# First stage of a two-layer diffusion backbone: filter spectra in float32, squares summed on four strips, the norm of x applied apart from its modulation, loads in another order

## The chip, the cores and the metric

The kernel runs on one core of a Trainium2 chip. The metric is device time in microseconds of one execution, the median of several runs. A core has TensorE (PE in the views, with its weight loads as PEld), VectorE (DVE), ScalarE (ACT), GpSimd (POOL) and the DMA engines, which SyncE's queue (SP) and POOL's queue feed. PE writes to PSUM; DVE and ACT read PSUM and SBUF, POOL reads SBUF.

## The reference

Two layers over 512 latent tokens (`x`) and 256 context tokens (`ctx`), width 1024. Layer 0 is differential attention with an MLP, layer 1 a Hyena long convolution with an MLP. All is float32. Cut to what the first stage prepares:

```python
silu_c = jax.nn.silu(c)
mod_l = jnp.split((silu_c @ w_mod[i] + b_mod[i])[:, None, :], N_MOD, axis=-1)
u_l = modulate(rms_norm(h_lat, norm_mix_pre[i]), mod_l[0], mod_l[1])   # x*(1+scale)+shift
u_c = modulate(rms_norm(h_ctx, norm_mix_pre[i]), mod_c[0], mod_c[1])
y_l, y_c = differential_attention(u_l, u_c, ...)                       # layer 0
...
h = (hdn @ w_out).reshape(n, 2, D_MODEL)                               # filters of layer 1
h = h * jnp.exp(-t * deltas[None, :])[:, None, :]
kf = jnp.fft.rfft(kern, n=2 * n, axis=0)                               # their spectra
```

## The kernel before

Weights and activations that PE multiplies are split in a high and a low float32r half (`split`, L259 to L263: ACT writes the high half by a cast on L262, DVE or POOL the difference on L263), and `mm3` makes three products of them. The string `WLO` names for each kind of weight which engine takes the difference, "v" for DVE and "p" for POOL, in turn.

The first stage is the function `startup` (L436 to L650). Its steps are named by a letter: `F0` to `F2` the small filter network, `f` the filters of 512 channels by 128 positions (`filters`), `s` the four spectra (`spectra`, two halves each), `m` eight products of the modulation row (`mod0`), `n` squares and norms (`norms`), `x` and `c` the eight modulated and split rows of x and of ctx (`modsplit`). `SORDER` sets the order in which the steps are recorded, before and after the modulation vectors `mod` and `modc` are there; `DORDER` sets the order of the loads on SP. Of a tile with a tag there are as many buffers as `bufs` says (`mw0` has 8, so four steps of `mod0`; the PSUM tag `ps` has 5).

A scheduler then places every recorded instruction on its engine; the table `PRI` shifts the priority of each named part of the program, in all stages. Each engine works strictly in the order it was given.

Then come `proj_q` (its products are `ps_q`), `proj_k` (`ps_k`), `proj_kc` (`ps_kc`) and `values` (`ps_v`) of attention. `ps_q`, `ps_k`, `ps_kc` and `ps_v` take turns in two PSUM buffers (tag `pj`), so `ps_kc` needs the buffer of `ps_q` and `ps_v` that of `ps_k`. A buffer is free when `rotate` has read it, at last by `rr<-ps_q` on DVE (L677), which needs the table `rope`. `rope` and the loads `mw` of `mod_step` (256 KB each, two buffers, consumed by `macc` on DVE, L361 and L363) lie in memory that the first stage gives back with its last instruction on DVE, `nlam` (L650). Behind attention follow the MLP of layer 0, the Hyena layer and its MLP.

Of the kernel before, what the change touches and what calls it, by code (L numbers as in the profile page):

```python
# [32 lines left out]
for _name, _w in (  # L33
# [38 lines left out]
 'b.hid': -65,
 'b.mod': 207,
 'b.pre': -127,
 'b.res': -60,
 'b.wload': -203,
 'e.cbc': -258,
# [3 lines left out]
 'e.hid': 73,
 'e.mod': 178,
 'e.pre': 0,
 'e.res': 575,
 'e.wload': -370,
 'f.cbc': 20,
# [12 lines left out]
 'h.pre': 492,
 'h.res': 7,  # L100
 'h.tr': 238,
 'h.wload': 122,
 'hid': -139,
# [1 line left out]
 'm.hid': 0,
 'm.wload': 29,
 'res': -163,
 'rot': 0,
 's.chain': 60,
 's.wload': 40,  # L110
 'smx': 6,
 'val': -198,
 'wload': -209,
 'wpart': 74,
 'wt': 328}
WLO = dict(fil="vp", fdft="ppv", start="p", q="vpv", k="pv", v="p", wo0="vvp", wo7="v", wo1="vpp", w1f0="vpv", w1f1="vvvp", w1_0="vpv", w1_1="vvvp", w2_0="v", w2_1="vpp", w2l0="v", w2l1="vpp", hin0="pvv", hin="pvp", hout="pv")
# [116 lines left out]
class K:  # L233
# [202 lines left out]
    def startup(self, sp, pp, cp):  # L436
# [104 lines left out]
        hs, hdif = {}, {}  # L541

        def filters(g, tt):

            gs = slice(512 * g, 512 * g + 512)
            if tt == 0:
                if g:
                    room = [sp.tile([P, 2, 512], F32R, tag="mw0", name="hs", bufs=MW0) for _ in range(8)]
                    room = [[room[i // 2][:, i % 2] for i in range(j, j + 4)] for j in (0, 4, 8, 12)]
                else:  # L550
                    room = [sp.tile([P, 4, 512], F32R, tag="hs" + t, name="hs") for t in "hl"] + [
                        cp.tile([P, 4, 512], F32R, tag="c" + t, name="hd") for t in "hl"]
                    room = [[t[:, i] for i in range(4)] for t in room]
                hs[g], hdif[g] = room[0:2], room[2:4]
            dec = sp.tile([P, 512], F32, tag="dec", name="dec", bufs=2)
            nc.scalar.activation(dec, dlt[:, gs], AF.Exp, scale=tn[:, tt:tt + 1])
            for i, dst in ((0, hs[g]), (1, hdif[g])):
# [4 lines left out]
                self.split(ht, dst[0][tt], dst[1][tt], self.turn("fil"))

        def spectra(g, m):
            ms = slice(P * m, P * m + P)
            for cs, src in ((0, hs[g]), (1, hdif[g])):
                so = self.wp.tile([P, 2, 512], F32, tag=("whi", "wlo")[cs], name="so")
                pe = pp.tile([P, 512], F32, tag="ps", name="ps_e")
                po = pp.tile([P, 512], F32, tag="ps", name="ps_o")
                for par, ps in ((0, pe), (1, po)):  # L570
# [2 lines left out]
                ev = sp.tile([P, 512], F32, tag="ev", name="ev", bufs=4)
                nc.scalar.copy(ev, pe)
                eng = nc.vector
                if g:
                    ov = sp.tile([P, 512], F32, tag="ev", name="ov", bufs=4)
                    nc.scalar.copy(ov, po)
                    eng, po = nc.gpsimd, ov
                eng.tensor_add(so[:, 0], ev, po)  # L580
                if cs == 0:
                    eng.tensor_sub(so[:, 1], ev, po)
                else:
                    eng.tensor_sub(so[:, 1], po, ev)
                nc.gpsimd.dma_start(self.spec[m][g][:, 2 * cs:2 * cs + 2], so)
# [699 lines left out]
```

## Time and profile before

| | us |
|---|---|
| median of 3 runs (1501.72 to 1508.04) | 1502.05 |
| the profiled execution, its own time | 1503.08 |
| span of that execution, first to last instruction | 1501.3 |
| PE busy (94% of the span) | 1411.0 |
| DVE busy (64%) | 967.6 |
| ACT busy (44%) | 665.9 |
| POOL busy (21%) | 321.2 |

The time lies 1.8 us above the span and 1.0 above the median. A busy PE is not PE at its peak: the span of a matmul in the views covers its latency, so the price of one in a stream is read from the distance of two starts. Times within the span start at its first instruction.

### The profile page before, as it was taken

The page shows a single profiled execution, that of the slowest core. Times are in us where ns is not written, and L with a number is a line of the kernel's source. Part 1 is how long each engine was busy: PE and PEld are TensorE (multiplying, and loading weights), DVE is VectorE, ACT ScalarE, POOL GpSimd, SP SyncE. Part 2 cuts the span into 40 slices and gives each one's busy share as a digit, 9 for nine tenths or more (in the row PEclk, how much of TensorE's full clock was granted, in tenths as well). Part 3 has the DMA queues.
Part 4 walks back from the last instruction along what each step waited for, and adds up shares of the span by engine and source line. Part 5 has one row for each costly group of instructions (what it writes and reads, how often), then busy time and mean ns, then how long its engine had stood idle before and what let it go on. Part 6 is the DMA issues. An engine that isn't in the chain of part 4 may idle for free. (4 is left out here: it accounts for less than half of the span.)

```text
span 1501.3 us, 21240 instructions
## 1 busy us (share of the span) xinstructions
PE 1411.0 (94%) x8248; PEld 1218.3 (81%) x8248; DVE 967.6 (64%) x1658; ACT 665.9 (44%) x1175; POOL 321.2 (21%) x207
## 2 busy tenths in 40 slices
PE   6979999999997999999999999999999899999996
PEld 1559797878887988888888888888989788888896
DVE  5887887878577864656555686999787323233334
ACT  4555757567554543313222355443554423142332
POOL 2351201120213101010100224323422212131121
PEclk9989999999998999999999999999999999999998
DMA  9332232130142275655454022322321422222201
GB/s 332 154 126 99 85 113 85 65 104 29 55 170 99 86 239 195 211 196 181 151 179 149 29 85 91 134 71 99 113 75 53 141 98 98 84 99 99 98 29 57
DMA packets 58144, 174.76 MB, mean 116 GB/s; under 512 B 5787, under 2 KB 15387, under 8 KB 57788
## 3 DMA queue, kind: packets, MB, share of 16 engines
q1 hardware_dynamic: 56892, 169.22, 32.9%
q0 software_dynamic: 1152, 4.19, 0.7%
q8 instruction: 65, 1.06, 0.3%
q14 instruction: 35, 0.29, 0.1%
HBM read 167.10 MB, written 6.29 MB: 115 GB/s over the span
## 5 line engine op out<-in xcount | busy, mean ns | idle before, releaser
L263 POOL TENSOR_TENSOR wlo<-raw,whi 128x1024 fp32r<-128x1024 f32 x43 | 120.7, 2808 | 552.4 <-ACT whi L262 483.5
L262 ACT CAST whi<-raw 128x1024 fp32r<-128x1024 f32 x99 | 104.1, 1052 | 194.3 <-PE ps L285 98.6
L262 ACT CAST wxhi<-raw 128x1024 fp32r<-128x1024 f32 x92 | 96.8, 1052 | 204.4 <-PE ps L285 174.4
L263 POOL TENSOR_TENSOR wxlo<-raw,wxhi 128x1024 fp32r<-128x1024 f32 x33 | 80.4, 2438 | 299.6 <-ACT wxhi L262 299.6
L363 DVE SCALAR_TENSOR_TENSOR macc<-mw,silu,macc 128x1024 f32<-128x1024 f32 (+1 forms) x91 | 100.2, 1101 | 27.9 <-DMA mw<-in_wmod_dram 27.0
L263 DVE TENSOR_TENSOR wxlo<-raw,wxhi 128x1024 fp32r<-128x1024 f32 x59 | 73.3, 1243 | 63.2 <-ACT wxhi L262 63.1
L263 DVE TENSOR_TENSOR wlo<-raw,whi 128x1024 fp32r<-128x1024 f32 x56 | 69.6, 1243 | 66.6 <-ACT whi L262 66.5
L285 PE MATMUL ps<-hl,wxhi 128*128 128x512 f32 x240 | 95.7, 399 | 0.0
L286 PE MATMUL ps<-hh,wxlo 128*128 128x512 f32 x240 | 95.7, 399 | 0.0
L284 PE MATMUL ps<-hh,wxhi 128*128 128x512 f32 x240 | 95.4, 398 | 0.0
L284 PE MATMUL ps<-uh,wxhi 128*128 128x512 f32 x240 | 94.9, 396 | 0.0
L286 PE MATMUL ps<-uh,wxlo 128*128 128x512 f32 x240 | 94.7, 394 | 0.0
L285 PE MATMUL ps<-ul,wxhi 128*128 128x512 f32 x240 | 94.4, 393 | 0.0
L262 ACT CAST hh<-relu 128x512 fp32r<-128x512 f32 (+1 forms) x80 | 42.1, 536 | 78.5 <-DVE relu L947 78.2
L985 DVE TENSOR_TENSOR y<-y,ps 128x512 f32<-128x512 f32 x32 | 22.0, 686 | 82.1 <-PE ps L286 82.1
L263 DVE TENSOR_TENSOR hl<-relu,hh 128x512 fp32r<-128x512 f32 (+1 forms) x80 | 56.8, 718 | 27.4 <-ACT hh L262 27.0
L284 PE MATMUL ps_h<-uh,wxhi 128*128 128x256 f32 x240 | 68.5, 289 | 4.6 <-DVE relu L947 2.2
L947 DVE SCALAR_TENSOR_TENSOR relu<-ps,relu 128x512 f32<-128x512 f32 x48 | 33.0, 687 | 56.2 <-ACT relu L946 56.2
L815 ACT ACTIVATE p<-sc,mx 128x768 f32<-128x768 f32 x64 | 57.8, 905 | 24.6 <-DVE mx L813 22.1
L285 PE MATMUL ps_h<-ul,wxhi 128*128 128x256 f32 x240 | 68.4, 286 | 0.0
L286 PE MATMUL ps_h<-uh,wxlo 128*128 128x256 f32 x240 | 68.1, 285 | 0.0
L813 DVE TENSOR_REDUCE mx<-sc 128x1 f32<-128x768 f32 x64 | 60.8, 952 | 2.7 <-PE sc L810 1.8
(364 smaller groups left out, 4559.2 us busy)
## 6 DMA issues: line engine op xcount, KB each, us to landing
raw<-in_w_dram SPq DMA_DIRECT2D x128, 512.0 KB, 3.2
mw<-in_wmod_dram SPq DMA_DIRECT2D x72, 512.0 KB, 4.4
mw<-in_wmod_dram SPq DMA_DIRECT2D x48, 256.0 KB, 2.9
raw<-in_hin_dram SPq DMA_DIRECT2D x24, 512.0 KB, 3.2
raw<-in_wo_dram SPq DMA_DIRECT2D x11, 512.0 KB, 3.2
spec<-so POOLq DMA_DIRECT2D x8, 512.0 KB, 2.9
raw<-in_wq_dram SPq DMA_DIRECT2D x8, 512.0 KB, 3.2
raw<-in_wk_dram SPq DMA_DIRECT2D x8, 512.0 KB, 3.2
```

The source lines that it names most:

```text
L262: self.nc.scalar.copy(hi, src)
L263: (eng or self.nc.vector).tensor_sub(lo, src, hi.bitcast(F32))
L284: mm(ps, lhi, rhi, start=(start and i == 0), stop=False)
L285: mm(ps, lhi, rlo, start=False, stop=False)
L286: mm(ps, llo, rhi, start=False, stop=(stop and i == n - 1))
L363: nc.vector.scalar_tensor_tensor(acc, w, self.silu[:, kc:kc + 1], acc, op0=ALU.mult, op1=ALU.add)
L813: nc.vector.tensor_reduce(mx, sc[:, 0:768], axis=AX.X, op=ALU.min)
L815: nc.scalar.activation(p, sc[:, 0:768], AF.Exp, scale=-1.0, bias=mx, accum_out=s1 if mp else s0[:, qb:qb + 1])
L947: nc.vector.scalar_tensor_tensor(r[:, 0:n], ps, 0.0, r[:, 0:n], op0=ALU.max, op1=ALU.mult)
L985: nc.vector.tensor_add(y[:, mt], y[:, mt], ps)
```

## The change

Filters and spectra are kept in float32: `filters` writes `hs` straight from PSUM, `dft` is loaded without a split, and each spectrum takes 8 float32 products where it took 24 of float32r halves. The sums and differences `so` are all on DVE, from PSUM. The squares of x and ctx go to PE by 24 products with a matrix of ones on four strips of 32 columns (`bcs`), ACT copies the strips to `rows`, and the six products of `rstd` sum them; the tree of DVE additions goes. x and ctx are multiplied by the reciprocal norm as soon as it is there, before the modulation is; `modsplit` then has two ACT instructions and a subtraction on DVE. `mw0` has 6 buffers. The tables `PRI`, `WLO`, `DORDER` and `SORDER` change, those of `PRI` and `WLO` in all stages.

```diff
-WLO = dict(fil="vp", fdft="ppv", start="p", q="vpv", k="pv", v="p", wo0="vvp", wo7="v", ... w1f0="vpv", w1f1="vvvp", ... hin0="pvv", hin="pvp", hout="pv")
+WLO = dict(fil="pp", fdft="vvpp", start="p", q="v", k="v", v="v", wo0="vvp", wo7="pvp", ... w1f0="vv", w1f1="vvvvp", ... hin0="vvvv", hin="vvv", hout="vvpv")
-DORDER = "zfwvdmlmxmDymcmmimm"
+DORDER = 'fzwivylxdcDmmmmmmmm'
+XU = "a"
-SORDER = ("F0 F1 F2 f00 f01 f02 m0 n f03 n s0 n m1 s0 s1 m2 f10 m3 n m4 f11 s1 m5 m6 m7".split(),
-          "f12 x1 x3 f13 x6 x2 x5 x4 c5 x0 s2 x7 c1 c0 c7 c3 s2 c6 s3 c2 s3 c4".split())
+SORDER = ("F0 F1 F2 n m0 n f00 f02 n n f03 f01 s1 m1 m4 s0 m3 m2 s0 f10 f11 m5 m6 m7 f13 f12".split(),
+          "x0 x4 x6 x3 s1 x2 s2 x5 x1 c6 c4 s2 c2 x7 s3 c0 s3 c1 c3 c7 c5".split())
-MW0 = 8
+MW0 = 6
...
-                raw = self.wp.tile([P, 1024], F32, tag="raw", name="raw", bufs=RAW)
-                dma(raw, ap["dft"][:, 1024 * i:1024 * i + 1024])
-                self.split(raw, *[d[:, i].rearrange("p a b c -> p (a b c)") for d in dft], self.turn("fdft"))
+                dma(dft[:, i].rearrange("p a b c -> p (a b c)"), ap["dft"][:, 1024 * i:1024 * i + 1024])
...
-                ht = sp.tile([P, 512], F32, tag="ev", name="ht", bufs=4)
-                nc.vector.tensor_mul(ht, pf, dec)
-                self.split(ht, dst[0][tt], dst[1][tt], self.turn("fil"))
+                nc.vector.tensor_mul(hs[g][:, i, tt], pf, dec)
...
-                    self.mm3(ps, [(dft[0][:, par, cs, t2, ms], dft[1][:, par, cs, t2, ms],
-                                   src[0][2 * par + t2], src[1][2 * par + t2]) for t2 in range(2)])
+                        for t2 in range(2):
+                            nc.tensor.matmul(ps, dft[:, par, cs, t2, ms], hs[g][:, cs, 2 * par + t2],
+                                             start=(t2 == 0), stop=(t2 == 1))
...
-                for n in (4, 2, 1):
-                    nc.vector.tensor_add(sq[:, 0:n], sq[:, 0:n], sq[:, n:2 * n])
+                    for k in range(KT):
+                        i = 32 * (k % 4)
+                        nc.tensor.matmul(bcs[i:i + 32, c0 + t0:c0 + t1], self.ones[:, 0:32], sq[:, k, t0:t1],
+                                         start=(k < 4), stop=(k >= 4), tile_position=(0, i))
...
-            self.rstd(pp, lambda b: sqs[b // 2][1][:, 0, P * (b % 2):P * (b % 2) + P], 768, 1.0 / D, tag="ps", bc=bcs)
-            nc.scalar.copy(bcc, bcs[:, T:T + TC])
+                nc.scalar.copy(rows, bcs)
+                self.rstd(pp, rows, 768, 1.0 / (32 * D), tag="ps", bc=bcs)
+                for k in range(KT):
+                    nc.vector.tensor_mul(xt[:, k], xt[:, k], bcs[:, 0:T])
+                for k in range(KT):
+                    nc.vector.tensor_mul(ct[:, k], ct[:, k], bcs[:, T:T + TC])
...
-            nc.vector.scalar_tensor_tensor(x, x, a, bc, op0=ALU.mult, op1=ALU.mult)
-            nc.scalar.activation(hi, x, AF.Identity, bias=s)
-            eng.scalar_tensor_tensor(lo, x, s, hi.bitcast(F32), op0=ALU.add, op1=ALU.subtract)
+            nc.scalar.activation(hi, x, AF.Identity, scale=a, bias=s)
+                nc.scalar.activation(x, x, AF.Identity, scale=a, bias=s)
+            nc.vector.tensor_sub(lo, x, hi.bitcast(F32))
```

How the change moves instructions is shown at three places. First SP's queue at the start; `xt` is x in halves, `ct` the context, `mw` the weights of the modulation. Before:

```order
L470 DMA zf<-in_zf_dram 33x576
L470 DMA fsm<-in_fsm_dram 128x136
L459 DMA fwo<-in_fwo_dram 64x1024 x2
L471 DMA vecs<-in_vecs_dram 128x313
L472 DMA dlt<-in_deltas_dram 128x1024
L454 DMA mw_103<-in_wmod_dram 128x1024
L454 DMA mw_104<-in_wmod_dram 128x1024
L472 DMA lam<-in_lam_dram 64x4
L454 DMA mw_108<-in_wmod_dram 128x1024
L454 DMA mw_109<-in_wmod_dram 128x1024
L468 DMA xt<-in_xT_dram 128x8x256
```

and after, from the same place:

```order
L467 DMA fwo<-in_fwo_dram 64x1024 x2
L477 DMA ident<-in_ident_dram 128x128
L477 DMA vecs<-in_vecs_dram 128x313
L474 DMA xt<-in_xT_dram 128x8x256
L478 DMA lam<-in_lam_dram 64x4
L474 DMA xt<-in_xT_dram 128x8x256
L478 DMA dlt<-in_deltas_dram 128x1024
L478 DMA ct<-in_cT_dram 128x2048
L471 DMA dft<-in_dft_dram 128x1024 x2
L462 DMA mw_109<-in_wmod_dram 128x1024
```

All of x and ctx and the transform's matrix now stand ahead of the sixteen loads `mw`.

Second, PE's queue where the modulation is made (`ps_m`, transposed to `ps_mt`) and up to the first product of attention. Before, `ps_mt` is followed by the rest of the filters, 48 products of spectra, and the first products `ps_q` and `ps_k` mixed:

```order
L617 MATMUL ps_mt_479<-ident,row_477 128x128 x4
L559 MATMUL ps_hf<-fwo,h_160 128x512 x3
L284 MATMUL ps_e<-hs,dfth 128x512
L285 MATMUL ps_e<-hs,dfth 128x512
L286 MATMUL ps_e<-hs,dftl 128x512
...
L646 MATMUL ps_l<-lp,ones 128x2
L284 MATMUL ps_q<-uh,whi 128x512
L284 MATMUL ps_k<-uh,whi 128x512
```

and after, from the last modulation products on:

```order
L504 MATMUL ps_m_150<-mw_137,rep 32x512 x2
L504 MATMUL ps_m_150<-mw_138,rep 32x512 x2
L561 MATMUL ps_hf<-fwo,h_153 128x512 x4
L624 MATMUL ps_mt_429<-ident,row_427 128x128 x4
L574 MATMUL ps_e<-hs,dft 128x512 x2
L574 MATMUL ps_o<-hs,dft 128x512 x2
...
L655 MATMUL ps_l<-lp,ones 128x2
L292 MATMUL ps_q<-uh,whi 128x512
```

All filters now stand ahead of `ps_mt`, and 20 products of spectra (five times the pair of rows shown) between it and `ps_l`.

Third, DVE's queue from the end of the first stage (`nlam`) on. Before:

```order
L650 SCALAR_TENSOR_TENSOR nlam<-le 128x1
L677 TENSOR_TENSOR rr<-ps_q,rope 128x512
L678 TENSOR_TENSOR sw<-sw,rope 128x512
L679 TENSOR_TENSOR rr<-rr,sw 128x512
L361 TENSOR_SCALAR macc<-mw,silu 128x512
L363 SCALAR_TENSOR_TENSOR macc<-mw,silu,macc 128x512
L677 TENSOR_TENSOR rr<-ps_k,rope 128x512
```

and after:

```order
L659 SCALAR_TENSOR_TENSOR nlam<-le 128x1
L271 TENSOR_TENSOR wlo<-raw,whi 128x1024
L369 TENSOR_SCALAR macc<-mw,silu 128x512
L371 SCALAR_TENSOR_TENSOR macc<-mw,silu,macc 128x512 x2
L271 TENSOR_TENSOR wlo<-raw,whi 128x1024
L371 SCALAR_TENSOR_TENSOR macc<-mw,silu,macc 128x512
L686 TENSOR_TENSOR rr<-ps_q,rope 128x512
L687 TENSOR_TENSOR sw<-sw,rope 128x512
L371 SCALAR_TENSOR_TENSOR macc<-mw,silu,macc 128x512
L688 TENSOR_TENSOR rr<-rr,sw 128x512
L750 SCALAR_TENSOR_TENSOR q_583<-rr,q_583 64x512
L371 SCALAR_TENSOR_TENSOR macc<-mw,silu,macc 128x512 x2
```

Four `macc` and two splits of weights now stand ahead of `rr<-ps_q`, and three more `macc` ahead of `rr<-ps_k`, which is the row after the last one shown.

## Rows read from the trace of the kernel before

**Rows 1.** Busy time by stretch: us, PE, PEld, DVE, ACT, POOL, clock, DMA share, GB/s.

```profile
0.00:87.00 87.00, 62.85 (x228) 31.18 (x228) 64.77 (x105) 44.27 (x70) 35.16 (x30) 0.92 0.59 222
...
6.00:36.00 30.00, 20.38 (x52) 6.28 (x52) 18.84 (x37) 15.91 (x24) 9.03 (x4) 0.89 0.97 370
...
109.00:470.00 361.00, 341.58 (x2291) 306.42 (x2290) 284.42 (x517) 223.25 (x406) 68.82 (x40) 0.99 0.26 87
...
900.00:1140.00 240.00, 226.70 (x1508) 207.29 (x1507) 203.57 (x362) 116.45 (x245) 83.39 (x41) 0.99 0.29 97
```

**Rows 2.** PE in order of time: start, us, instruction, and idle time before it.

```profile
87.29 0.77 PE L284 MATMUL ps_q<-uh,whi 128*128 128x512 f32 x1 [5.87 <-DVE xt L628]
...
102.47 0.28 PE L284 MATMUL ps_kc<-ch,whi 128*128 128x256 f32 x1
...
108.43 0.58 PE L284 MATMUL ps_v<-whi,ch 128*128 128x256 f32 x1 [2.92 <-DVE rr L677]
```

**Rows 3.** DVE and POOL in order of time, 82 to 87 us.

```profile
82.76 0.73 DVE L628 SCALAR_TENSOR_TENSOR xt<-xt,a_l,ps_bcs 128x512 f32<-128x512 f32 x1
83.41 3.07 DVE L630 SCALAR_TENSOR_TENSOR ul<-xt,mod,uh 128x512 fp32r<-128x512 f32 x1
...
83.43 1.28 POOL L580 TENSOR_TENSOR so<-ev,ov 128x512 f32<-128x512 f32 x1
```

**Rows 4.** ACT and PE in order of time, from the first filter to the modulation.

```profile
19.23 1.72 ACT L532 ACTIVATE h<-arg 64x256 f32<-64x256 f32 x4 [2.39 <-DVE arg L525]
...
20.25 9.94 PE L559 MATMUL ps_hf<-fwo,h 128*128 128x512 f32 x16 [3.10 <-DVE h L535]
...
58.41 2.78 PE L497 MATMUL ps_m<-mw,rep 128*32 128x512 f32 x22
...
62.07 0.60 PE L617 MATMUL ps_mt<-ident,row 128*128 128x128 f32 x4
```

**Rows 5.** PE's weight loads in order of time: two neighbours in float32, two in float32r.

```profile
27.46 0.19 PEld L559 LDWEIGHTS ps_hf<-fwo,h 128*128 128x128 f32 x1 [0.24 <-issue]
27.89 0.19 PEld L559 LDWEIGHTS ps_hf<-fwo,h 128*128 128x128 f32 x1 [0.24 <-issue]
...
44.29 0.19 PEld L285 LDWEIGHTS ps_e<-hs,dfth 128*128 128x128 f32 x1
44.52 0.19 PEld L286 LDWEIGHTS ps_e<-hs,dftl 128*128 128x128 f32 x1
```

**Rows 6.** ACT's groups by shape, 0 to 96 us: count, busy us, mean ns, idle before.

```profile
L629 ACT ACTIVATE uh<-xt,mod 128x512 fp32r<-128x512 f32 x8 | 5.5, 721 | 2.9 <-DVE xt L628 2.7
L574 ACT COPY ev<-ps_e 128x512 f32<-128x512 f32 x8 | 4.7, 581 | 5.4 <-PE ps_e L286 2.0 <-POOL so L582 1.6 <-POOL so L584 1.5
...
L629 ACT ACTIVATE ch<-ct,modc 128x256 fp32r<-128x256 f32 x8 | 3.7, 504 | 6.1 <-DVE ct L628 5.9
```

**Rows 7.** DVE and SP in order of time, at the end of the first stage.

```profile
96.01 0.15 DVE L650 SCALAR_TENSOR_TENSOR nlam<-le 128x1 f32<-128x1 f32 x1
...
96.37 0.33 SPq L657 DMA_DIRECT2D rope<-in_rope_dram  x1
```

**Rows 8.** DMA issues: count, size, median us from issue to landing.

```profile
mw<-in_wmod_dram SPq DMA_DIRECT2D x48, 256.0 KB, 2.9
...
rope<-in_rope_dram SPq DMA_DIRECT2D x1, 512.0 KB, 3.4
```

**Rows 9.** Groups by shape, first two of 109 to 470 us, the others 900 to 1140.

```profile
L263 POOL TENSOR_TENSOR wlo<-raw,whi 128x1024 fp32r<-128x1024 f32 x13 | 32.3, 2484 | 196.9 <-ACT whi L262 139.7 <-issue 28.0 <-PE ps_kc L286 20.4
L263 DVE TENSOR_TENSOR wlo<-raw,whi 128x1024 fp32r<-128x1024 f32 x12 | 14.6, 1219 | 2.4 <-ACT whi L262 2.3
...
L263 POOL TENSOR_TENSOR wlo<-raw,whi 128x1024 fp32r<-128x1024 f32 x13 | 47.8, 3676 | 109.9 <-ACT whi L262 105.5 <-DVE ql L263 4.4
...
L1085 DVE SCALAR_TENSOR_TENSOR x<-z,vecs,x 128x512 f32<-128x512 f32 x12 | 14.9, 1248 | 0.3
...
L1212 DVE SCALAR_TENSOR_TENSOR vx<-vx,vecs,ps_y 128x512 f32<-128x512 f32 x8 | 5.9, 740 | 0.0
```

More of the change, by code (lines that the diff above doesn't have):

```diff
@@ L55 @@
  'a.chain': 0,
- 'a.css': 31,
+ 'a.css': 97,
  'a.hn': 0,
- 'a.mod': -11,
+ 'a.mod': 0,
  'a.pk': 0,
  'a.pkc': 0,
- 'a.pq': 0,
- 'a.rot': 58,
- 'a.smx': -20,
+ 'a.pq': 190,
+ 'a.rot': 261,
+ 'a.smx': -16,
  'a.val': 20,
- 'a.wload': 6,
- 'a.wpart': -855,
+ 'a.wload': -354,
+ 'a.wpart': -466,
  'a.wt': 40,
- 'b.cbc': 0,
+ 'b.cbc': 244,
  'b.chain': 60,
- 'b.css': 4,
+ 'b.css': 0,
  'b.halves': 0,
[L72 to L77, printed above, removed]
+ 'b.hid': 0,
@@ L78 @@
+ 'b.mod': -9,
+ 'b.pre': -129,
+ 'b.res': -42,
+ 'b.wload': -661,
+ 'e.cbc': 92,
  'e.chain': 1498,
- 'e.css': 28,
+ 'e.css': -1173,
  'e.halves': 0,
[L81 to L86, printed above, removed]
+ 'e.hid': 63,
+ 'e.mod': -184,
+ 'e.pre': -214,
+ 'e.res': -51,
+ 'e.wload': 0,
+ 'f.cbc': -35,
  'f.chain': -96,
- 'f.css': 52,
+ 'f.css': 297,
  'f.halves': 0,
- 'f.res': 6,
+ 'f.res': 35,
  'f.wload': 324,
- 'h.cbc': 328,
- 'h.chain': 250,
- 'h.css': -153,
+ 'h.cbc': 298,
@@ L95 @@
+ 'h.chain': 246,
+ 'h.css': -162,
  'h.dft': 111,
- 'h.fconv': 11,
- 'h.halves': 0,
+ 'h.fconv': 90,
+ 'h.halves': 55,
  'h.idft': 0,
[L99 to L103, printed above, removed]
- 'm.halves': 0,
[L105 to L116, printed above, removed]
+ 'h.pre': 227,
@@ new lines @@
+ 'h.res': 0,
+ 'h.tr': 207,
+ 'h.wload': -275,
+ 'hid': 0,
+ 'm.halves': 0,
+ 'm.hid': 1,
+ 'm.wload': 67,
+ 'res': -338,
+ 'rot': 176,
+ 's.chain': -20,
+ 's.css0': 0,
+ 's.fil': 0,
+ 's.mod0': 0,
+ 's.ms': 0,
+ 's.net': 0,
+ 's.norm': 0,
+ 's.spec': 0,
+ 's.wload': 129,
+ 'smx': -2,
+ 'val': -359,
+ 'wload': -5,
+ 'wpart': 20,
+ 'wt': 120}
+WLO = dict(fil="pp", fdft="vvpp", start="p", q="v", k="v", v="v", wo0="vvp", wo7="pvp", wo1="vvp", w1f0="vv", w1f1="vvvvp", w1_0="vpv", w1_1="vvvp", w2_0="vvv", w2_1="vvvp", w2l0="vv", w2l1="vv", hin0="vvvv", hin="vvv", hout="vvpv")
@@ L447, in startup @@
         dlt = sp.tile([P, D], F32, name="dlt")
-        dft = [sp.tile([P, 2, 2, 2, 256], F32R, name="dft" + t) for t in "hl"]
+        dft = sp.tile([P, 2, 2, 2, 256], F32, name="dft")
         lam = sp.tile([64, 4], F32, name="lam")
@@ L493, in startup @@
         pm = pp.tile([P, 512], F32, tag="pm", name="ps_m0", bufs=1)
+        @within("mod0", self)
         def mod0(kc):
@@ L507, in startup @@
         tn = sp.tile([P, 4], F32, name="tn")
+        @within("net", self)
         def network(layer):
@@ L539, in network @@
             nc.vector.scalar_tensor_tensor(tn, h2[:, 1, 508:512], 0.0, tneg, op0=ALU.mult, op1=ALU.add)
-        hs, hdif = {}, {}
+        hs = {}
+        @within("fil", self)
         def filters(g, tt):
@@ L546, in filters @@
             if tt == 0:
[L547 to L553, printed above, removed]
@@ L564, in spectra @@
         def spectra(g, m):
             ms = slice(P * m, P * m + P)
[L566 to L570, printed above, removed]
-                    self.mm3(ps, [(dft[0][:, par, cs, t2, ms], dft[1][:, par, cs, t2, ms],
-                                   src[0][2 * par + t2], src[1][2 * par + t2]) for t2 in range(2)])
[L573 to L585, printed above, removed]
@@ new lines, in spectra @@
+            for cs in range(2):
+                with self.pri("spec"):
+                    so = self.wp.tile([P, 2, 512], F32, tag=("whi", "wlo")[cs], name="so")
+                    pe = pp.tile([P, 512], F32, tag="ps", name="ps_e")
+                    po = pp.tile([P, 512], F32, tag="ps", name="ps_o")
+                    for par, ps in ((0, pe), (1, po)):
+                        for t2 in range(2):
+                            nc.tensor.matmul(ps, dft[:, par, cs, t2, ms], hs[g][:, cs, 2 * par + t2],
+                                             start=(t2 == 0), stop=(t2 == 1))
+                    ev = sp.tile([P, 512], F32, tag="ev", name="ev", bufs=2)
+                    nc.scalar.copy(ev, pe)
+                    nc.vector.tensor_add(so[:, 0], ev, po)
+                    if cs == 0:
+                        nc.vector.tensor_sub(so[:, 1], ev, po)
+                    else:
+                        nc.vector.tensor_sub(so[:, 1], po, ev)
+                    nc.gpsimd.dma_start(self.spec[m][g][:, 2 * cs:2 * cs + 2], so)
@@ L612, in startup @@
         self.first = [self.wload(ap[w][0], "start") for w in ("wq", "wk")]
-        row = sp.tile([P, 512], F32, tag="ev", name="row0", bufs=4)
+        row = sp.tile([P, 512], F32, tag="row0", name="row0")
         nc.scalar.copy(row, pm)
```

28 lines of the change are left out of this document (16 added, 12 removed).

## The prediction

> **What bounds the kernel now.** I read the busy time by stage first. PE is busy for 342 of 361 us in attention and 227 of 240 in the Hyena layer, but only for 63 of the first 87 [rows 1]: a quarter of the first stage is empty, and that is what the change touches most. Then PE in order of time: its first product of attention starts at 87.29, after 5.87 us of waiting for DVE's rows of x; `ps_kc` follows at 102.47, and `ps_v` only at 108.43, having waited 2.92 us for `rr`, DVE's rotation, to give a PSUM buffer back [rows 2]. From `ps_v` on, the PE work of the two kernels is the same and nearly in the same order, so I take the start of `ps_v` as the point at which the first stage is compared.
>
> Why DVE is late with x is seen where POOL works too: a subtraction with both inputs in SBUF that starts 0.02 us before POOL's sum `so` takes 3.07 us, while the product `xt` of the same size, which reads the norm from PSUM, takes 0.73 [rows 3].
>
> **First stage: to the first filter.** The squares of ctx now stand ahead of `h` in ACT's queue, and ctx comes later in the queue of loads. Ahead of and with ctx go 4.57 MB, of which the first 0.9 are there by about 6 us; the rest at 370 GB/s [rows 1] takes 9.9, to 15.9. Two squares (an estimate of 1.1 each, twice a copy of 512 columns [rows 6]) and the four sines, 1.72 [rows 4], end at about 20, or 21.5 if the loads are less dense. I take 21; before it was 20.95. So the new order of loads gains nothing here, and x, ctx and the transform cost nothing either; the 24 products for the squares lie in the time in which PE waits for `h`, whatever one costs up to some 0.3 us.
>
> **PE from there to attention.** A float32 product of 512 columns is two instructions 0.43 us apart, so 0.86; three of float32r halves are 0.69 [rows 5]. The new queue holds 16 products of filters and 32 of spectra: 48 x 0.86 = 41.3. The first eight run partly at the lower clock (1.2 of 2.4 GHz; the stage's mean is 0.92 of full [rows 1]): they took 9.94 us before [rows 4] instead of 6.9, so +3.0. 32 products of the modulation at 2 x 2.78/22 = 0.25 [rows 4] are 8.1. Six transposes of norms, four of the modulation at 0.15 [rows 4] and six small ones are 2. Sum 54.4. The last six loads `mw` need buffers that PE frees at about 45; 3.1 MB at 370 GB/s land at some 54, a microsecond after PE wants them: +1. So `ps_q` starts at 21 + 55.4 = 76.4, against 87.29.
>
> The spectra alone cost PE 32 x 0.86 - 96 x 0.23 = 5.4 us more than before. What goes for them are 16 splits of filters and two of the transform on ACT, DVE and POOL, the tree of additions, and POOL's part in `so`.
>
> **Does x arrive in time?** 20 products of spectra, 17.2 us, lie between the modulation (`ps_mt`, at 58.8; before 62.07 [rows 4]) and `ps_q`. From 59.8 on, ACT has 16 rows of x at 0.72, 16 of ctx at 0.50 and five copies at 0.58 [rows 6]: 22.4, to 82.2. The eighth row of x is done at about 76, and PE wants it at 76.4 + 21 x 0.23 = 81.2. DVE's subtractions are not slowed, since POOL has no sums left. So `ps_q` and `ps_k`, 48 x 0.23 = 11 us, run without a stop to 87.4; before, `ps_kc` started at 102.47: 15 us earlier.
>
> **Where half of it goes.** `ps_kc` needs the buffer of `ps_q`. The table `rope` may be loaded only behind `nlam`, which now follows the last row of ctx: 83; before 96.01, with the load issued 0.36 later [rows 7]. It lands 3.4 us after its issue [rows 8], at 86.7. Ahead of `rr<-ps_q` on DVE now stand four `macc`. The first two loads `mw` follow `rope` at once (87.0, 87.7); the third can go out only when the first `macc` (0.5 us) has freed its buffer, at 87.5, and takes 2.9 to 3.4 us [rows 8], to 90.6; its `macc` (0.7, as the product `xt` [rows 3]) ends at 91.3, the split (1.22 [rows 9]) at 92.5, the fourth at 93.2, `rr` at 93.9. So `ps_kc` starts at 94, after a wait of 6.6, and while DVE waits there the rest of the rotation and SP's loads behind the freed buffers wait too. Three more `macc` stand ahead of `rr<-ps_k`; the seventh load lands at about 99 by the same steps (two buffers, some 3.8 us for a pair), and `ps_v` starts at 100.5. Against 108.43 that is **-8**. The bounds: with no wait at all `ps_v` would start at 87.4 + 2.9 = 90.3 (-18), and with each load 1 us slower at about 104 (-4).
>
> **The other stages.** The tables move splits from POOL to DVE. By the order of both kernels POOL keeps 3 of 16 in attention and 2 of 17 in the Hyena layer: 28 x 1.22 = 34 us more for DVE. On POOL one takes 2.48 us in attention and 3.68 in the Hyena layer [rows 9], and slows DVE meanwhile: the Hyena layer's `x` products with two SBUF inputs take 1.25 us on average, those with a PSUM input 0.74 [rows 9], so 12 of them alone lose 6 us. For one split DVE's gain lies between nothing and POOL's whole duration, so its balance lies between -1.22 and +1.3 (attention) or +2.5. I take zero for DVE, being about midway. A weight's buffer comes back 1.3 to 2.5 us sooner, and PE's idle time in both stages is 19.4 + 13.3 us [rows 1], of which only a few microseconds wait for weights: **-3**, between -16 and +20 (below). The rest I leave at zero: outside these two and the first 87 us PE is busy for 780 of 813 us (1411.0 less the three of [rows 1]).
>
> **Sum.** The profiled execution took 1503.08: 1503.1 - 8 - 3 = 1492.1. The median of the runs shown is 1.0 lower, so 1491.
>
> **The rivals.**
> Without the wait. If `macc` gets its loads sooner than the steps above say, `ps_kc` follows `ps_k` almost at once and `ps_v` starts near 94.5, -14: 1485. For it: the loads are short and the queue is otherwise empty then; against it: two buffers, and SP's order.
>
> DVE set free. Suppose every split on POOL held DVE for its whole duration: 13 x 2.48 + 13 x 3.68 = 80 us for 26 of them, against 32 for doing them on DVE, so 48 us of DVE come back; if that removes half of the 32.7 us for which PE idles in the two stages, 16 go instead of 3: 1478. For it is the 3.07 [rows 3]; against it, DVE's mean in the Hyena layer is only 0.51 over the undisturbed one, and in attention DVE is 79% busy, so that a good part of POOL's work meets a DVE that idles or reads PSUM. The Trainium skill, "SBUF — State Buffer", section "Who interferes with whom", has this rule: a DVE instruction with two SBUF inputs and a GpSimd one that reads SBUF exclude each other, and the one that issues second "fully blocks". By that rule alone the time is this rival's 1478; the trace agrees on one pair (3.07 with two sums of 1.28 beside it), but the mean of 1.25 shows that few instructions meet a split.
>
> The modulation is late. If PE's wait for the last `mw` is not 1 but 7 us (six buffers instead of eight, and SP waits for PE at each), everything behind moves with it: 1497. For it: ten of the sixteen loads wait for PE; against it: 370 GB/s.
>
> Slower: DVE becomes the bound. The 34 us of splits fall on an engine that is busy for 79% of attention and 85% of the Hyena layer [rows 1]. If what POOL held up does not come back and 60% of the 34 reach PE through rotations and the products of the Hyena layer, 20 are lost: 1503.1 - 8 + 20 - 1 = 1514. It decides from 8 us on. Against it are the slow instructions of [rows 3, 9].
>
> **How the numbers follow.** The forecast has 0.45 (its own range 1486 to 1496), without the wait 0.20, DVE set free 0.10, late modulation 0.15, DVE the bound 0.07; 0.03 is for what I have not thought of. A measurement of this kernel tells about 0.5%, 7.5 us, from no change. Below 1494.5 lie the second and third case and most of the first: faster 0.70; within 0.5% the fourth and the rest of the first, 0.23; slower 0.07. The range reaches from the third case's 1479 to 1500, which leaves out the slower one and a tenth at the low end.
>
> **What would show it.** In the profile after: `ps_q` at 76 (73 to 80) with little idle time before it; `uh` rows on ACT from 60 without waiting for DVE; `ul` at 0.7 each; PE idle ahead of `ps_kc` for 5 to 8 us and released by `rr`, with `macc` waiting for DMA on DVE; `ps_v` at 100.5. PE's idle time in attention within a few microseconds of 19.4. I am wrong if `ps_q` starts after 82, if `ps_kc` follows `ps_k` at once, or if attention or the Hyena layer is over 8 us longer or shorter than before.

## The result, and the profile after

The changed kernel takes 1465.06 us (median of 4 runs, 1464.36 to 1466.66) against 1503.47 for the kernel before on the same chip: the ratio is 0.9741, 95% interval 0.9717 to 0.9766. The prediction was 1491, between 1479 and 1500: the sign was right, the gain of 38 us more than three times the 11 forecast, and the time lies outside the range. The profiled execution took 1465.16 us.

The head of the page after (share of the span, then the number of instructions):

```profile
span 1463.4 us, 21191 instructions
PE 1400.8 (96%) x8264; PEld 1203.8 (82%) x8264; DVE 937.9 (64%) x1698; ACT 663.5 (45%) x1169; POOL 160.3 (11%) x140
```

Of the 37.9 us by which the span is shorter, PE's idle time gives 27.7 (span less busy time: 90.3 before, 62.6 after) and PE's busy time 10.2, although its work grew by the float32 spectra: the mean granted clock rose from 0.977 to 0.990.

To see where, the program is cut at three places where both kernels have done nearly the same PE work: the start of `ps_v`, the end of the last `ps_w` (attention's output projection) and the end of the last `ps_y` (the Hyena layer's inverse transform). Lengths in us:

| | to `ps_v` | to the last `ps_w` | to the last `ps_y` | to the end |
|---|---|---|---|---|
| before | 108.4 | 340.0 | 620.2 | 432.7 |
| after | 101.0 | 330.9 | 606.6 | 424.9 |
| difference | -7.4 | -9.1 | -13.6 | -7.8 |

The first stage gave what was forecast for it (-8); the stages behind it gave 30.5 instead of 3. The last three stages by busy time (us, PE, PEld, DVE, ACT, POOL, clock, DMA share, GB/s), first before:

```profile
108.40:448.40 340.00, 324.19 (x2154) 289.22 (x2155) 268.07 (x483) 215.04 (x388) 58.62 (x31) 0.99 0.26 87
448.40:1068.60 620.20, 595.23 (x3458) 524.69 (x3457) 432.66 (x719) 240.46 (x433) 120.44 (x84) 0.98 0.40 136
1068.60:1502.00 433.40, 411.98 (x2341) 359.68 (x2339) 186.62 (x330) 154.90 (x266) 97.83 (x57) 0.98 0.25 88
```

and after:

```profile
101.00:432.00 331.00, 319.68 (x2155) 287.55 (x2156) 263.57 (x489) 214.26 (x388) 33.18 (x21) 1.00 0.26 86
432.00:1038.50 606.50, 591.19 (x3458) 520.10 (x3457) 424.73 (x740) 241.69 (x436) 61.27 (x64) 0.99 0.42 139
1038.50:1464.00 425.50, 408.95 (x2340) 357.27 (x2339) 191.32 (x344) 153.24 (x262) 55.09 (x40) 0.99 0.27 90
```

POOL's busy time halves; DVE's falls by 7.7 us over the three (887.4 to 879.6), though it took over splits from POOL. They are counted in the groups of the whole span (L271 is L263 of before; count, busy us, mean ns):

```profile
L271 DVE TENSOR_TENSOR wlo<-raw,whi 128x1024 fp32r<-128x1024 f32 x91 | 111.9, 1230 | 110.7 <-ACT whi L270 105.3 <-PE ps_h L293 5.3
...
L271 DVE TENSOR_TENSOR wxlo<-raw,wxhi 128x1024 fp32r<-128x1024 f32 x73 | 90.0, 1233 | 81.3 <-ACT wxhi L270 81.2
...
L271 POOL TENSOR_TENSOR wxlo<-raw,wxhi 128x1024 fp32r<-128x1024 f32 x19 | 45.5, 2397 | 310.5 <-ACT wxhi L270 310.5
...
L271 POOL TENSOR_TENSOR wlo<-raw,whi 128x1024 fp32r<-128x1024 f32 x8 | 19.7, 2462 | 303.9 <-ACT whi L270 303.9
```

and before:

```profile
L263 POOL TENSOR_TENSOR wlo<-raw,whi 128x1024 fp32r<-128x1024 f32 x43 | 120.7, 2808 | 552.4 <-ACT whi L262 483.5 <-issue 35.4 <-PE ps_kc L286 20.4
...
L263 POOL TENSOR_TENSOR wxlo<-raw,wxhi 128x1024 fp32r<-128x1024 f32 x33 | 80.4, 2438 | 299.6 <-ACT wxhi L262 299.6
L263 DVE TENSOR_TENSOR wxlo<-raw,wxhi 128x1024 fp32r<-128x1024 f32 x59 | 73.3, 1243 | 63.2 <-ACT wxhi L262 63.1
L263 DVE TENSOR_TENSOR wlo<-raw,whi 128x1024 fp32r<-128x1024 f32 x56 | 69.6, 1243 | 66.6 <-ACT whi L262 66.5
```

So 49 splits went over, two of them ahead of `ps_v`: 47 x 1.23 = 58 us were added to DVE in these three stages, and it is busy for less. Its other instructions took 66 us less; six of them moved ahead of `ps_v`, which is some 4 us of that, and the rest became shorter.

One place shows it, at the start of layer 0's MLP, where DVE's queue is the same in both kernels and PE waits for a sum of squares. DVE, POOL and PE in order of time, before:

```profile
451.42 1.22 DVE L263 TENSOR_TENSOR wxlo<-raw,wxhi 128x1024 fp32r<-128x1024 f32 x1
452.56 3.11 DVE L343 TENSOR_TENSOR nacc<-nacc,nsq 128x256 f32<-128x256 f32 x2
...
452.52 2.34 POOL L263 TENSOR_TENSOR wxlo<-raw,wxhi 128x1024 fp32r<-128x1024 f32 x1 [1.47 <-ACT wxhi L262]
...
455.72 0.77 PE L314 MATMUL ps_s<-ones,nacc 128*128 128x1 f32 x4 [3.64 <-DVE nacc L343]
```

and after:

```profile
434.72 1.22 DVE L271 TENSOR_TENSOR wxlo<-raw,wxhi 128x1024 fp32r<-128x1024 f32 x1
435.85 0.95 DVE L351 TENSOR_TENSOR nacc<-nacc,nsq 128x256 f32<-128x256 f32 x2
...
436.85 0.61 PE L322 MATMUL ps_s<-ones,nacc 128*128 128x1 f32 x4 [1.54 <-DVE nacc L351]
```

The two additions read two SBUF tiles each. Beside a split on POOL they took 3.11 us instead of 0.95, and PE's wait is 2.10 longer: the hold-up passed to PE whole. Over the whole span, PE's waits for `nacc` fell from 11.3 to 8.2 us.

The rows that answer to [rows 2], PE in order of time:

```profile
83.28 0.80 PE L292 MATMUL ps_q<-uh,whi 128*128 128x512 f32 x1 [4.89 <-ACT le L657]
...
96.62 0.28 PE L292 MATMUL ps_kc<-ch,whi 128*128 128x256 f32 x1
...
101.02 0.39 PE L292 MATMUL ps_v<-whi,ch 128*128 128x256 f32 x1 [1.37 <-DVE rr L686]
```

`ps_q` starts 7 us later than forecast, `ps_kc` follows `ps_k` at once, and `ps_v` is within 0.5 us of the forecast; how that fits together is told below.

### The profile page after: what moved, and what is told of

It reads as the page before. It is cut to its first block, busy times and chain, and to the rows that moved or that the text cites. A ratio compares the mean times of both kernels' runs of the same rounds, so it can differ in the third digit from the quotient of the medians.

```text
span 1463.4 us, 21191 instructions
## 1 busy us (share of the span) xinstructions
PE 1400.8 (96%) x8264; PEld 1203.8 (82%) x8264; DVE 937.9 (64%) x1698; ACT 663.5 (45%) x1169; POOL 160.3 (11%) x140
## 4 chain that ended last, share of the span: by engine, by line
PE 70%; DVE 12%; ACT 6%; DMA 3%; issue 2%; POOL 1%; DVEq 0%; SPq 0%; ACTq 0%; POOLq 0%
PE ps L292 12%; PE ps L293 12%; PE ps L294 12%; PE ps_h L292 4%; PE ps_h L294 4%; PE ps_h L293 4%; ACT sw L684 2%; DVE wlo L271 1%; DMA mw<-in_wmod_dram 1%; PE ps_z L292 1%; PE ps_z L293 1%; PE ps_z L294 1%; DVE hT L913 1%; PE sc L818 1%; PE ps_v L293 1%
## 5 line engine op out<-in xcount | busy, mean ns | idle before, releaser
L270 ACT CAST wxhi<-raw 128x1024 fp32r<-128x1024 f32 x92 | 96.6, 1050 | 213.2 <-PE ps L293 172.2
L271 DVE TENSOR_TENSOR wlo<-raw,whi 128x1024 fp32r<-128x1024 f32 x91 | 111.9, 1230 | 110.7 <-ACT whi L270 105.3
L271 DVE TENSOR_TENSOR wxlo<-raw,wxhi 128x1024 fp32r<-128x1024 f32 x73 | 90.0, 1233 | 81.3 <-ACT wxhi L270 81.2
L371 DVE SCALAR_TENSOR_TENSOR macc<-mw,silu,macc 128x1024 f32<-128x1024 f32 (+1 forms) x91 | 96.1, 1056 | 23.5 <-DMA mw<-in_wmod_dram 22.8
L271 POOL TENSOR_TENSOR wxlo<-raw,wxhi 128x1024 fp32r<-128x1024 f32 x19 | 45.5, 2397 | 310.5 <-ACT wxhi L270 310.5
L271 DVE TENSOR_TENSOR hl<-relu,hh 128x512 fp32r<-128x512 f32 (+1 forms) x80 | 47.5, 602 | 25.3 <-ACT hh L270 25.2
L292 PE MATMUL ps<-hh,whi 128*128 128x512 f32 x144 | 57.1, 398 | 0.6 <-ACT hh L270 0.6
L293 PE MATMUL ps<-hl,whi 128*128 128x512 f32 x144 | 56.9, 396 | 0.1
```

What stands on the lines that cost most here:

```text
L270: self.nc.scalar.copy(hi, src)
L271: (eng or self.nc.vector).tensor_sub(lo, src, hi.bitcast(F32))
L292: mm(ps, lhi, rhi, start=(start and i == 0), stop=False)
L293: mm(ps, lhi, rlo, start=False, stop=False)
L371: nc.vector.scalar_tensor_tensor(acc, w, self.silu[:, kc:kc + 1], acc, op0=ALU.mult, op1=ALU.add)
```

## Experiments: which part did it

The change has three parts that can be taken apart: the first stage, the engines of the splits behind it (`WLO`), and the priorities behind it (`PRI`). With before and after these runs make all eight combinations.

**The splits alone.** The table of the change for all weights behind the first stage, in the kernel before:

```diff
-WLO = dict(... q="vpv", k="pv", v="p", ... hin0="pvv", hin="pvp", hout="pv")
+WLO = dict(... q="v", k="v", v="v", ... hin0="vvvv", hin="vvv", hout="vvpv")
```

> The kernel before, with only the table of split engines (WLO) of the change, for the weights of all stages behind the first. The change as a whole gave 1503.5 to 1465.1, of which 7.4 us lie ahead of the first product ps_v and about 30 behind it. Theory A (splits on POOL hold up DVE, and their removal gives DVE time back): most of the 30 comes from this table alone: 1503.5 - 25 = 1478, with DVE's product x with two SBUF inputs in the Hyena layer back at about 0.75 us from 1.25. Theory B (the other priorities do it, the table moves DVE's balance by about zero as the prediction took it): 1500, within 4 of before. If DVE became the bound without the new priorities (the prediction's rival): above 1506.

1490.86, ratio 0.9929 (0.9908 to 0.9950): between the two. The product x did fall to 745 ns, as A said (before: 1248 [rows 9]):

```profile
L1085 DVE SCALAR_TENSOR_TENSOR x<-z,vecs,x 128x512 f32<-128x512 f32 x12 | 8.9, 745 | 0.1
```

**Splits and priorities, without the first stage.** The kernel before with both tables:

```diff
- 'a.wload': 6,
+ 'a.wload': -354,
...
- 'b.wload': -203,
+ 'b.wload': -661,
...
- 'h.wload': 122,
+ 'h.wload': -275,
```

> The kernel before with the table of split engines and the priorities of the change in all stages behind the first; the first stage stays as it was. If the gain of 30 us behind ps_v is made there: 1465.1 + 7.4 = 1472.5, within 2. If it hangs on the new first stage (another phase of loads and splits): clearly above, 1480 to 1495.

1475.12, ratio 0.9823 (0.9808 to 0.9838): 10 us above the changed kernel, between the two expectations and nearer to the first.

**The change without the splits**, its `WLO` put back behind the first stage:

> The changed kernel with the old table of split engines behind the first stage (new first stage and new priorities). Theory A: the gain of the splits goes, 1465.1 + 25 = 1490. Theory B: 1468.

1517.51, ratio 1.0106 (1.0084 to 1.0127). Both theories were wrong: the other two parts together make the kernel slower than before, and the table of splits is worth 52 us here.

**The change without the priorities**, the entries of `PRI` behind the first stage put back:

> The changed kernel with the old priorities behind the first stage (new first stage and new split engines). Theory A: 1465.1 + 5 = 1470. Theory B: 1465.1 + 27 = 1492.

1483.65, ratio 0.9886 (0.9867 to 0.9904): 18.6 above the changed kernel, again between the two.

**The first stage alone:**

> The first stage of the change alone: old split engines and old priorities behind it. The prediction's term for the first stage is -8 (between -18 and -4): 1494.5. The two traces have ps_v 7.4 us earlier: 1495 if the rest keeps it. If the change as a whole is needed for it to arrive at the end: 1500 or above.

1504.71, ratio 1.0021 (1.0011 to 1.0030): no gain at all. `ps_v` is 4.7 us earlier, and attention 6.4 longer.

**The priorities alone:**

> The kernel before with the new priorities of all stages behind the first, alone. With the new first stage and the old split engines they gave 1517.5, where the new first stage alone gave 1504.7: 12.8 more. Theory I (the new priorities put a weight's load and split late and need the short split on DVE): slower than before again, 1508 to 1520. Theory J (the loss came from the new first stage and the priorities together): 1495 to 1503.

1521.38, ratio 1.0133 (1.0102 to 1.0164), theory I, by a little more than it said.

The eight times side by side (us, medians; before is that of the runs beside the first stage alone and beside the priorities alone; beside the splits alone it was 1502.5):

| | old splits | new splits | splits are worth |
|---|---|---|---|
| old first stage, old priorities | 1502.0 | 1490.9 | -11 |
| new first stage, old priorities | 1504.7 | 1483.7 | -21 |
| old first stage, new priorities | 1521.4 | 1475.1 | -46 |
| new first stage, new priorities | 1517.5 | 1465.1 | -52 |

The priorities cost 13 to 19 us with the old splits and give 16 to 19 with the new ones; the first stage costs 3 or gives 4 with the old splits, and gives 7 to 10 with the new. No part has a price of its own that can be summed. By stage, at the same three cuts:

| | to `ps_v` | to the last `ps_w` | to the last `ps_y` | to the end |
|---|---|---|---|---|
| splits alone | 106.2 | 351.5 | 608.0 | 425.4 |
| splits and priorities | 105.3 | 333.4 | 606.9 | 426.5 |
| first stage alone | 103.7 | 346.4 | 619.3 | 433.1 |
| priorities alone | 106.4 | 350.7 | 624.6 | 433.8 |
| no splits | 105.0 | 349.3 | 626.7 | 433.0 |
| no priorities | 102.2 | 343.6 | 607.7 | 428.3 |

Behind attention the splits decide: with them on DVE the last two stages take 1033 to 1036 us (after: 1031.5), without 1052 to 1060 (before: 1052.9), whatever the rest. In attention neither table helps alone: only with both is it shorter than before.

## Experiments: why the splits matter

**POOL reads beside DVE.** The changed kernel, with scraps on POOL where the old table had its splits; `WLO0` is the old table:

```diff
-        self.split(raw, hi, lo, self.turn(cat))
+        e = self.turn(cat)
+        self.split(raw, hi, lo, e)
+        if e is self.nc.vector and WLO0[cat][self.wn[cat] % len(WLO0[cat])] == "p":
+            for j in range(3):
+                self.nc.gpsimd.tensor_sub(self.junk, hi[:, 320*j:320*j+320].bitcast(F32), hi[:, 320*j+64:320*j+384].bitcast(F32))
```

> The changed kernel, with its splits where they are (on DVE); where the old table would have had POOL, POOL now also subtracts three pieces of 320 columns of the high half from each other into a scrap that nobody reads (53 times three). The other engines' order is the same. It adds work and leaves nothing out. Theory A (a POOL instruction on SBUF holds up DVE's instructions with two SBUF inputs): DVE's splits and other such instructions beside the scraps become longer, their sum over the undisturbed rises from 28 us to 60 or more, and the time to 1480 to 1500. Theory L (what mattered is only that POOL's split is late, 2.5 to 3.7 us instead of 1.2, so that PE and the loads wait): 1465 within 3, since nobody waits for the scrap.

1511.17, ratio 1.0053 (1.0036 to 1.0070): 46 us more than the changed kernel, above theory A's range; L falls. DVE is busy for 992.4 us instead of 937.9, with the same instructions in the same order:

```profile
PE 1420.2 (94%) x8264; PEld 1219.5 (81%) x8264; DVE 992.4 (66%) x1698; ACT 664.9 (44%) x1169; POOL 367.0 (24%) x299
```

It has now both costs, its own splits and the hold-ups, and so ends above the kernel before.

**POOL writes beside DVE.** The same places, about the same POOL time, but nearly nothing read:

```diff
-            for j in range(3):
-                self.nc.gpsimd.tensor_sub(self.junk, hi[:, 320*j:320*j+320]..., hi[:, 320*j+64:320*j+384]...)
+            self.nc.gpsimd.tensor_sub(self.junk[:, 0:1], hi[:, 0:1].bitcast(F32), hi[:, 64:65].bitcast(F32))
+            for j in range(9):
+                self.nc.gpsimd.memset(self.junk, 1.0)
```

> As the run with the scraps that POOL subtracts (1511.2), at the same 53 places, but POOL now fills the scrap nine times with a constant: it writes 2880 columns and reads one. The other engines' order is again that of the changed kernel. The Trainium skill, page SBUF — State Buffer, section Who interferes with whom, says that a DVE instruction with two SBUF inputs contends with a GpSimd instruction that reads SBUF and not with one that only writes. By that rule the time is 1465 to 1470, and DVE's excess stays near 28 us. If it is POOL's mere activity that holds DVE up (any access, or what waits behind it in POOL's queue): 1490 or more, in proportion to POOL's busy time.

1471.11, ratio 0.9792 (0.9774 to 0.9810). POOL is busier than with the reads (384.7 us against 367.0) and than in the kernel before (321.2), yet DVE is at 941.3 and the time only 6 us above the changed kernel:

```profile
PE 1405.5 (95%) x8264; PEld 1209.1 (82%) x8264; DVE 941.3 (64%) x1698; ACT 663.4 (45%) x1169; POOL 384.7 (26%) x670
```

Groups of the Hyena layer, with the scraps that read:

```profile
L289 POOL TENSOR_TENSOR junk<-whi 128x320 f32<-128x320 f32 x35 | 59.2, 1692 | 85.5 <-ACT whi L271 83.7
...
L1100 DVE SCALAR_TENSOR_TENSOR vx<-zz,vecs,vx 128x512 f32<-128x512 f32 x4 | 7.2, 1814 | 0.0
...
L1227 DVE SCALAR_TENSOR_TENSOR vx<-vx,vecs,ps_y 128x512 f32<-128x512 f32 x8 | 5.9, 738 | 0.0
```

with the scraps that write:

```profile
L290 POOL MEMSET junk<- 128x320 f32 x135 | 49.4, 366 | 7.6
...
L1228 DVE SCALAR_TENSOR_TENSOR vx<-vx,vecs,ps_y 128x512 f32<-128x512 f32 x8 | 5.9, 740 | 0.5 <-PE ps_y L300 0.5
...
L1101 DVE SCALAR_TENSOR_TENSOR vx<-zz,vecs,vx 128x512 f32<-128x512 f32 x4 | 2.9, 744 | 0.0
```

The product `vx<-zz,vecs,vx` reads two SBUF tiles: 1814 ns beside POOL's reads (a mean of four: 2.89, 2.88, 0.75 and 0.74 us), 744 beside its writes. This is the group of the layer that was held up most; all 48 products `x` and `vx` of its kind take 50.6 us with the reads, and 40.1 both with the writes and in the changed kernel. `vx<-vx,vecs,ps_y` reads one of them from PSUM: 738 and 740. That is the rule of the Trainium skill, "SBUF — State Buffer", section "Who interferes with whom", in both halves, and the prediction gave it a chance of 0.10. The writes still cost 6 us, and so may the reads, by whatever causes that; some 40 of the 46 are left for the reading. The cause of the 6 was not settled, but it looks common to both runs. PE waits for a difference of the transform's matrix, `idftl`, that POOL makes late behind the scraps, first with the reads, then with the writes; in the changed kernel it does not:

```profile
PE ps_y L298 <- POOL idftl L272: 2.3, 1, 2.3
...
PE ps_y L299 <- POOL idftl L272: 3.0, 1, 3.0
```

ACT waits for the scraps to let go of a high half, 14.5 us with the reads and 18.5 with the writes.

## Experiments: order and the first stage

**The weight loads' priorities.** The changed kernel with the nine entries `wload` behind the first stage put back (six of them differ; the lines above show three of them):

> The changed kernel with the old priorities of the weight loads alone (the entries wload behind the first stage). Old priorities for everything gave 1483.7. Theory T (the new priorities matter because a weight that is loaded and split later leaves DVE free for what is due, and that needs the short split on DVE): most of those 18.6 us come back, 1478 to 1484. If it is the other entries (rotation, softmax, chains): 1465 to 1470.

1491.46, ratio 0.9928 (0.9913 to 0.9943). Theory T, and more than it said: this alone costs 26 us, more than putting back all the priorities (18.6). Nearly all of it, 25 us, is in attention, which takes 355.8 us. PE's waits in attention (total us, times, longest), the changed kernel:

```profile
PE sc L818 <- ACT b L760: 1.9, 2, 1.7
```

and with the old entries:

```profile
PE sc L818 <- ACT b L760: 7.8, 6, 2.3
PE sc L818 <- ACT p L824: 3.5, 8, 1.2
```

The busy times of that stretch, with the clock behind the brackets:

```profile
100.80:456.60 355.80, 333.10 (x2153) 296.95 (x2154) 272.89 (x491) 212.79 (x387) 32.30 (x21) 0.96 0.25 82
```

The scores `sc` wait for the keys `b`, and PE's clock is 0.96 of full instead of 1.00: of the 25 us, 13.4 are PE's longer busy time (333.1 against 319.7), the rest idle time. Which of the six entries it is was not tried.

**The wait of `ps_q`.** In the changed kernel `ps_q` waits for `le`, the last instruction of the first stage on ACT. Its nine lines, from `lp` to `nlam`, are moved up unchanged:

```diff
+        lp = sp.tile([64, 2], F32, name="lp")
...
+        nc.vector.scalar_tensor_tensor(self.nlam, le[:, 1:2], -LAM_INIT, le[:, 0:1], op0=ALU.add, op1=ALU.subtract)
         self.first = [self.wload(ap[w][0], "start") for w in ("wq", "wk")]
```

> The changed kernel with the small product ps_l and its exponential le recorded before the two first weights, so that they are no longer the last ones on PE and ACT in the first stage. Theory Q (in the changed kernel ps_q waits 4.9 us for the PSUM that le, queued behind the 16 rows of ctx on ACT, gives back, and pays for it again by the lower clock): ps_q starts at 78.5 to 81 instead of 83.3, its 24 products take 5.5 us instead of 7.9, and rr, behind two macc instead of four, comes earlier too: ps_v at 95 to 97.5 instead of 101.0, time 1460. Theory R (the rotation waits for rope and macc anyway, so the wait only moves): ps_v at 100 to 101, time 1464 to 1465.

1484.74, ratio 0.9881 (0.9866 to 0.9895): 20 us slower than the changed kernel, which neither theory had. The first stage did get shorter: `ps_v` starts at 98.92, 2.1 earlier. But attention takes 350.3 us instead of 330.9. The scheduler had placed what follows otherwise: at 365 of the 1698 places of DVE's queue stands another instruction than in the changed kernel. PE and ACT in order of time at one of the places:

```profile
82.44 0.47 PE L292 MATMUL ps_q<-uh,whi 128*128 128x512 f32 x1 [2.80 <-DVE so L582]
...
242.85 0.79 PE L818 MATMUL sc<-b,q 128*128 128x512 f32 x1 [2.30 <-ACT b L760]
...
240.07 2.34 ACT L684 COPY sw<-ps_q 32x512 f32<-32x512 f32 x4 [0.80 <-PE ps_s L322]
242.43 0.37 ACT L760 CAST b<-ps_kc 64x256 fp32r<-64x256 f32 x1
```

Four copies of the next rotation now stand ahead of the last key on ACT, and PE waits 2.30 us for it; in the changed kernel all four `b<-ps_kc` stand ahead of those copies. The priorities were the same, but they are shifts against the place in the program, and this set was good for one program only: nine moved lines cost more than half of the change's gain.

**Still fewer splits on POOL.** Of the 27 left, those of `w1_1`, `w2_1` and `hout` (14, not the some 20 that the expectation names), and then also of `w1f1` and `w1_0` (nine more):

> The changed kernel with the weights of the last MLP, w2 of the first one and the Hyena output (w1_1, w2_1, hout) split on DVE alone: some 20 of the last splits leave POOL. DVE's excess from 1140 us on is 3.3 us in the changed kernel, and PE idles for 8 us there. Theory A: a little faster, 1462 to 1465. If DVE's own 1.2 us per split reach PE: 1466 to 1470.

> The kernel of the last run with the weights w1 of both MLPs on DVE alone as well (w1f1, w1_0, w1_1, w2_1, hout). The last run gave 1463.2, no measurable difference from the changed kernel. Of DVE's excess 9 us are left between the first MLP and the Hyena layer and 6 behind it. Theory A: 1460 to 1464. If the order that is planned anew from the first MLP on decides (42 rows of PE's queue stand elsewhere): anything up to 1470.

1463.22, ratio 0.9746 (0.9728 to 0.9764), and 1464.48, ratio 0.9742 (0.9725 to 0.9758): neither can be told from the changed kernel (0.9717 to 0.9766). No version of this study measurably beats it.

## Why the prediction was right and wrong

**First stage, to the modulation: right.** The first filter starts at 21.37 (forecast 21), `ps_mt` at 60.31 (58.8), PE's last product ahead of `ps_q` starts at 78.0 (the sum had them end at 76.4). ACT's rows of x and ctx run from 61.52 to 83.06 (59.8 to 82.2), and x is there in time. The 21 hit partly by its allowance for slower loads: ctx landed at 17.8, not at 15.9, and `h` then waited 0.50 us for DVE's `arg`, which the forecast did not have.

**`ps_q` at 76.4: wrong by 7 us.** The step "ps_q starts when the spectra are done and x is there" left out PSUM. It takes a bank of the first stage, and waits until those are read: on ACT at last by `le`, behind the rows of ctx (with `le` moved up the wait ended with `so`, DVE's last reader of them). ACT in order of time:

```profile
82.08 1.10 ACT L638 ACTIVATE ct<-ct,modc,a_c 128x256 f32<-128x256 f32 x2
83.06 0.17 ACT L657 ACTIVATE le<-ps_l 128x2 f32<-128x2 f32 x1
```

The trace of before held the hint: the 5.87 us of [rows 2] ended with DVE's last product `xt`, which reads the norm from PSUM; the prediction took it for a wait for x as data. After the wait the clock was low, so `ps_q` and `ps_k` were done at 96.6 instead of 87.4.

**`rr` at 93.9 and `ps_v` at 100.5: right, to 1.5 and 0.5 us.** DVE's chain behind the loads `mw` came as worked out, but later: the third load's `macc` starts at 91.99 instead of 90.6, and `rr` ends at 95.35 where the forecast has 93.9:

```profile
91.99 0.75 DVE L371 SCALAR_TENSOR_TENSOR macc<-mw,silu,macc 128x512 f32<-128x512 f32 x1 [2.41 <-DMA mw<-in_wmod_dram]
92.66 1.22 DVE L271 TENSOR_TENSOR wlo<-raw,whi 128x1024 fp32r<-128x1024 f32 x1
93.79 0.74 DVE L371 SCALAR_TENSOR_TENSOR macc<-mw,silu,macc 128x512 f32<-128x512 f32 x1
94.66 0.69 DVE L686 TENSOR_TENSOR rr<-ps_q,rope 128x512 f32<-128x512 f32 x1
```

The wait of 6.6 us that was forecast ahead of `ps_kc` was taken by `ps_q` instead, under the same chain. So -7.4 against -8 rests on the chain, and not on `ps_q`, which was wrong and lay under its cover: `rr` starts directly behind `macc`, 3.3 us after the last product of `ps_q` ended. That it came to 0.5 us is luck in part. The forecast has the seventh load set the time of `ps_v`; in the trace the last two `macc` ahead of `rr<-ps_k` waited for no load, DVE waited only 0.70 us ahead of them for ACT's `q`, and most of the 1.5 us came back. Of the rivals "without the wait" had `ps_kc` right and `ps_v` wrong; PE waited 0.67 us for a load `mw`, so the modulation was not late.

**That the first stage's 8 us reach the end: not so by themselves.** Alone, the new first stage gained nothing (1504.7). The prediction compared at `ps_v` because the PE work behind it is "nearly in the same order"; nearly was not enough.

**The other stages, -3 between -16 and +20: the step that failed; they gave -30.5.** Two things in it. First its count: it took the 28 splits of attention and the Hyena layer and left the rest at zero because PE is busy there for 780 of 813 us; in all 49 were moved, 17 of them in the stretch from the last `ps_y` on, which holds the Hyena output and the last MLP and gave 7.8 alone. Second its currency. That a split's balance on DVE is about zero was right: 58 us more of splits, DVE's busy time 7.7 lower. But the prediction let PE's waits follow that balance (zero for DVE, so that only the 3 us for weights that come back sooner are left), and the time does not follow the balance. A split on DVE lies where the scheduler put it; a hold-up by POOL falls on whatever DVE does just then, such as the two additions that PE waits for. Behind attention PE's busy time fell by 7.1 us and its idle time by 14.3, together 21.4, where DVE's busy time fell by 3.2.

The reverse run says the same: 54.5 us of hold-ups added to DVE cost 46 us of time.

**"DVE set free" (0.10, 1478): the right mechanism,** turned down because the mean in the Hyena layer was only 0.51 us over the undisturbed one. It was under-sized too: it gave back half of two stages' idle time, and counted neither the other stages nor the clock. Its 48 us for DVE were not what came: DVE's busy time behind the first stage fell by 7.7. **"DVE the bound" (0.07, 1514)**: attention does get longer when the splits come alone (351.5 instead of 340.0). That DVE bounds it there is not shown: it is busy for 275.0 of 351.4 us, before for 268.1 of 340.0, nearly the same share. The new priorities take the loss away, and no term of the prediction spoke of them. Why attention needs both was followed no further than to the `wload` entries; the places where the old ones cost most were not looked for. All three signs that the prediction named for being wrong came: `ps_q` after 82, `ps_kc` behind `ps_k` at once, and attention and the Hyena layer shorter by more than 8 us.

## To carry to other kernels

Where two engines exclude each other, price the hold-up by what it falls on, not by the sum of busy time: look at the instructions that the bound engine waits for, and see what the other engine runs beside them. A change of tables that were fitted together cannot be summed from its parts, and an edit of a few instructions ahead of a tuned order can cost more than the edit gains; compare orders first. When an engine waits at the border of two stages, ask which memory comes back there and who reads it last, before taking the wait for one on data.
